# Gate-up's two plain sets turned token-major, one small store moved, another scheduler model

## The chip, the cores and the metric

The kernel runs on one core of a Trainium2 chip. The metric is the device time of one launch in microseconds (us). Before the change three executions took 2731.93, 2734.11 and 2739.36 us; their median, 2734.11 us, is the number to beat. One further execution was profiled; its span, from the first to the last instruction, is 2731.7 us.

## The reference, cut to what matters

One decoder layer over 512 tokens of width 2048, in float32. Two token mixers (latent attention and a gated delta rule) come first. The change is in the channel mixer behind them:

```python
x = x + gt_a * mix
h = _rmsnorm(x, norm_ffn[l]) * (1.0 + sc_f) + sh_f
gate, up = jnp.split(h @ w_gate_up[l], 2, axis=-1)      # 5632 columns each
x = x + gt_f * ((jax.nn.silu(gate) * up) @ w_down[l])
return _rmsnorm(x, final_norm)
```

`gt_f` is a vector of 2048 gates, one per output channel.

## The kernel before, in words

**Precision.** Every product of two float32 matrices is made of three TensorE matmuls over operands split into a high and a low part (`fp32r`): high by high, high by low, low by high. ScalarE casts the high part (`hi`), VectorE subtracts to get the low part (`lo`), for weights and activations alike. `halves` (L263, L264) does it for plain weights, `hilo` (L239, L240) for activations.

**Order of the work.** A layer is a stream of `Unit`s, each with a load (SyncE's DMA queue), a split (ScalarE and VectorE), a list of matmuls, and hooks `pre` and `post`. `Driver.run` takes unit after unit; before a unit's matmuls (after them, where the unit is marked `late`) it splits the next ones, so that two split units lie ahead (`AHEAD`), and loads further ahead (`LOADS = 4` loaded units, 2 in the large sets). Beside the units run generators, called chains, that make the next stage's operands. After each `GROUP = 12` matmuls, each counted with its unit's `weight`, `pump` takes every chain one step further. `hold` at the end of a set delays that by one group. Instructions of SyncE, GpSimd and TensorE stay in program order (`PINNED`). VectorE's and ScalarE's order is chosen when the program is built, by a scheduler that plays the program through a timing model of its own.

**Buffers.** Tiles of 128 x 512 come from a pool of 68 slots (`S`), raw weights from 5 buffers of 128 x 1024, `hi` and `lo` from 4 each, and PSUM gives 8 banks of 128 x 512 float32.

**Gate-up.** The 5632 feature columns of gate and of up are cut into 11 x 512. The first 512 are two *plain* sets (`gu0`, `gu1`) of 256 gate columns and the 256 up columns that belong to them; the other ten are *large* sets (`big(s)`, s = 1 to 10), made with a Strassen-like scheme of seven products, `m1` to `m7`, over sums of weights and sums of activations.

- Input of all: `h2T[h][q]`, high and low part, for token halves h = 0, 1 (256 tokens) and q = 0 to 7 (two blocks of 128 of the 2048 input channels). The chain `h2_gen(h)` makes one q in two steps (L1752, L1753, then `hilo`); the one for h = 1 runs during `gu0`.
- `gu0` walks over the 16 channel blocks twice, once for each token half, loading and splitting its weights twice. It is feature-major: the weight block (128 x 128) is the stationary operand, the 256 tokens of a half the moving one, so each matmul has 256 columns; a bank holds 128 features x 512 tokens. `gu1` (`gu_both(1)`) walks once over the channel blocks and takes both token halves with each, again in matmuls of 256 columns. Each set has 384 matmuls.
- `gu_done` reads the banks at the end of a set: SiLU of the gate on ScalarE (L2152), times up on VectorE (L2154), into two tiles `sl`, which GpSimd's queue stores to `f_dram[s, h]`.
- During `gu1` the chain `combine` (L1780 and `hilo`) makes the sums of activations that the large sets need: for each of four q, four subtractions or additions and four splits. `comb[q]` is due at unit 2q of the first large set.
- A large set has 16 units. Units 0 to 7 run four products, units 8 to 15 the other three. Its matmuls are token-major: 128 tokens of an activation are stationary, 512 weight columns move, each matmul has 512 columns. Units 0 to 7 form sums of weights on VectorE (L1826, 128 x 1024 and 128 x 512) ahead of the split (L1847 on ScalarE, L1848 on VectorE) and store one of them to `s_dram`; units 8 to 15 load it again.
- A large set's result is token-major, but the down projection needs features on partitions. The result, four tiles in `turning`, is turned by TensorE during units 9 to 12 of the next set (`turned_a`: 16 transposes in four groups of four, one ScalarE copy per group at L1957, one store to `f_dram` per group). During the first large set `turning` is empty, and `turned_a` does nothing.

**The gate's store.** `side(g_dram..., gt_ffn)` writes the 2048 gates from a tile of 128 x 16 to memory, in an order in which no two neighbours of a partition are neighbours in memory: 4 bytes at a time. It is on GpSimd's queue, behind the unit stream's `gu1`. Its reader is a load at the kernel's very end (`row<-g_dram`).

Of the kernel before, what the change touches and what calls it, by code (L numbers as in the profile page):

```python
# [171 lines left out]
def block_kernel(ctx: ExitStack, tc: tile.TileContext, a: dict, out, out_t):  # L172
# [1967 lines left out]
    def gu_done(s, ps):  # L2140

        f = {}

        def done(j, h):
            if h == 0:
                return
            for h in range(2):
                fs, v = slice(256 * (j % 2), 256 * (j % 2) + 256), ps[j][:, 256 * h:256 * h + 256]
                if j < 2:
                    if j == 0:  # L2150
                        f[h] = S("sl")
                    nc.scalar.activation(f[h][:, fs], v, AF.Silu)  # L2152
                else:
                    nc.vector.tensor_tensor(f[h][:, fs], f[h][:, fs], v, ALU.mult)  # L2154
                if j == 3:
                    side(f_dram[s, h], f[h][:])
        return done

    def gu_both(s):

        st = {}

        def unit(k0):
            box = {}

            def start():
                box["raw"] = fetch(gu_loads(s)(k0, 2), 512, 2)

            def split():
                box["w"] = halves(box.pop("raw"), 512, 2)  # L2170

            def pre():
                if k0 == 0:
                    st["ps"] = [PS(f"gu{s}") for _ in range(4)]
                    st["done"] = gu_done(s, st["ps"])

            def after(j, h):
                st["done"](j, h)

            mms = []  # L2180
            for kk in range(2):
                k = k0 + kk
                for j in range(4):
                    for h in range(2):
                        for n, (wi, xi) in enumerate(((0, 0), (0, 1), (1, 0))):
                            mms.append(lambda kk=kk, k=k, j=j, h=h, n=n, wi=wi, xi=xi: mm(
                                st["ps"][j][:, 256 * h:256 * h + 256], box["w"][wi][:, kk, tok(j)], half_k(h2T[h][k // 2], k)[xi],
                                start=k == 0 and h == 0 and n == 0, stop=k == KT - 1 and n == 2, skip_group_check=True))
                        if k == KT - 1:
                            mms[-1] = lambda m=mms[-1], j=j, h=h: (m(), after(j, h))  # L2190
# [26 lines left out]
    def ffn():  # L2217
        def gu0():
            us, st = [], {}

            def done(ps):
                done_ = gu_done(0, ps)
                for j in range(4):
                    for h in range(2):
                        done_(j, h)

            for h in range(2):
                half = fm_set("gu0", gu_loads(0), 512, KT, lambda k, h=h: half_k(h2T[h][k // 2], k), done if h else None, st=st,
                              cols=slice(256 * h, 256 * h + 256), alone=True)
# [5 lines left out]
                us.append(half)  # L2235
# [6 lines left out]
            with_pre(us[0], start)  # L2242
            return us[0] + us[1]
# [285 lines left out]
```

## Time and profile before

| | |
|---|---|
| median of three executions | 2734.11 us (2731.93 to 2739.36) |
| profiled execution | span 2731.7 us |
| instructions | 41089, of which 15304 matmuls and as many weight loads |
| loads of `w_gate_up` in the large sets | 400 of 256 KB, 3.6 us from issue to landing (median) |
| stage of the plain sets | 1379.9 to 1473.4 us |
| the ten large sets | 1473.4 to about 2250 us |
| mean granted TensorE clock | 0.998 |

How to read it. "Busy" for the matmul engine (PE) includes modelled ends, so the pace of PE is better read from the chain of work that ended last: a row such as "start, duration, PE name xN" is N matmuls in a row, and duration over N is the pace. PE is TensorE's matmuls, PEld its weight loads, DVE VectorE, ACT ScalarE, POOL GpSimd, SP SyncE; a "q" behind a name is the engine's sequencer. In a table by stretches of time each row has a stretch, its length, the busy time (and count) of PE, PEld, DVE, ACT and POOL, the granted clock of TensorE as a share, the mean busy share of the 16 DMA engines, and GB/s moved. All matmuls are recorded at the line of a helper, L155, so they are told apart by the name of their output tile: `gu` for the plain sets, `m` for the products, `aT` for transposes.

### The profile page before, as it was taken

How to read it: one execution, taken by the hardware profiler on the slowest of the kernel's cores; microseconds unless marked ns; L12 is line 12 of the kernel's file. 1: busy time of each engine (PE TensorE's matmuls, PEld its weight loads, DVE VectorE, ACT ScalarE, POOL GpSimd, SP SyncE). 2: the span in 40 equal slices, each digit the busy share in tenths (PEclk: the TensorE clock that was granted, in tenths of full speed). 3: DMA queues.
4: the chain of work that ended last, by engine and by line, in shares of the span. 5: the costliest groups of instructions: out<-in, count | busy, mean ns of one | idle time of the engine just before them, and what ended most of it. 6: DMA issues, size and time to landing. Idle time of an engine off the chain costs nothing.

```text
span 2731.7 us, 41089 instructions
## 1 busy us (share of the span) xinstructions
PE 2705.7 (99%) x15304; PEld 2351.8 (86%) x15304; DVE 2098.3 (77%) x3361; ACT 1204.9 (44%) x1717; POOL 258.8 (9%) x361
## 2 busy tenths in 40 slices
PE   9999999999999999999999999999999999999998
PEld 7888788888888888889999888888888888998997
DVE  8784656677977886788787877778787777877877
ACT  3443432442344343234473444444444446446445
POOL 0000011102101000001000000000000103113113
PEclk9999999999999999999999999999999999999999
DMA  9896455646666978725854556665655668569565
GB/s 364 302 357 215 143 177 173 190 144 185 198 187 194 315 253 313 258 78 131 268 185 136 195 201 208 204 208 198 212 190 198 214 212 208 132 194 202 126 190 178
DMA packets 315489, 562.20 MB, mean 206 GB/s; under 512 B 40772, under 2 KB 120916, under 8 KB 315288
## 3 DMA queue, kind: packets, MB, share of 16 engines
q1 hardware_dynamic: 264776, 458.99, 51.6%
q0 software_dynamic: 31872, 74.76, 10.6%
q10 hardware_dynamic: 18640, 25.83, 2.7%
q8 instruction: 120, 1.97, 0.3%
q14 instruction: 81, 0.66, 0.1%
HBM read 476.62 MB, written 83.89 MB: 205 GB/s over the span
## 4 chain that ended last, share of the span: by engine, by line
PE 90%; DVE 4%; DMA 3%; issue 2%; ACT 1%; SPq 0%; DVEq 0%; ACTq 0%; POOL 0%
PE m L155 41%; PE gb L155 6%; PE v L155 4%; PE gu L155 3%; PE z L155 3%; PE ya L155 3%; PE k L155 3%; PE q L155 3%; PE yb L155 3%; PE dn L155 3%; PE s L155 3%; PE ckv L155 2%; PE cq L155 2%; PE wo L155 1%; PE qk L155 1%
## 5 line engine op out<-in xcount | busy, mean ns | idle before, releaser
L263 ACT CAST hi<-raw 128x1024 fp32r<-128x1024 f32 x249 | 258.8, 1041 | 538.9 <-DMA raw<-in_w_in_dram 164.9
L264 DVE TENSOR_TENSOR lo<-raw,hi 128x1024 fp32r<-128x1024 f32 x249 | 302.6, 1216 | 202.4 <-ACT hi L263 197.6
L1847 ACT CAST hi<-raws 128x512 fp32r<-128x512 f32 (+1 forms) x240 | 218.6, 911 | 328.0 <-PE m L155 269.2
L1848 DVE TENSOR_TENSOR lo<-raws,hi 128x512 fp32r<-128x512 f32 (+1 forms) x240 | 247.4, 1042 | 83.9 <-ACT hi L1847 83.6
L155 PE MATMUL m<-xh,lo 128*128 128x256 f32 x1088 | 308.4, 283 | 1.3 <-DVE lo L2023 1.3
L155 PE MATMUL m<-xh,hi 128*128 128x256 f32 x1088 | 308.1, 283 | 1.5 <-ACT hi L2022 1.5
L155 PE MATMUL m<-xl,hi 128*128 128x256 f32 x1088 | 307.9, 283 | 0.0
L449 DVE CUSTOM_DVE_ANT_0 rawm<-rawm,cbc 128x1024 f32<-128x1024 f32 x192 | 232.1, 1230 | 2.0 <-DMA rawm<-in_w_mod_dram 1.7
L155 PEld LDWEIGHTS m<-xh,lo 128*128 128x128 f32 x1088 | 208.8, 192 | 2.0 <-DVE lo L2023 1.9
L155 PEld LDWEIGHTS m<-xh,hi 128*128 128x128 f32 x1088 | 208.9, 192 | 1.7 <-ACT hi L2022 1.7
L155 PEld LDWEIGHTS m<-xl,hi 128*128 128x128 f32 x1088 | 208.9, 192 | 0.1
L155 PE MATMUL m<-hi,h2h 128*128 128x512 f32 x480 | 190.1, 396 | 0.0
L155 PE MATMUL m<-hi,h2l 128*128 128x512 f32 x480 | 187.2, 390 | 0.0
L155 PE MATMUL m<-lo,h2h 128*128 128x512 f32 x480 | 187.2, 390 | 0.0
L2022 ACT CAST hi<-sums 128x1024 fp32r<-128x1024 f32 x88 | 92.2, 1048 | 134.4 <-PE m L155 102.4
L2023 DVE TENSOR_TENSOR lo<-sums,hi 128x1024 fp32r<-128x1024 f32 x88 | 107.4, 1220 | 45.5 <-ACT hi L2022 45.4
L1847 ACT CAST hi<-sums 128x1024 fp32r<-128x1024 f32 x80 | 84.2, 1053 | 109.4 <-PE m L155 104.5
L1848 DVE TENSOR_TENSOR lo<-sums,hi 128x1024 fp32r<-128x1024 f32 x80 | 97.6, 1220 | 26.7 <-ACT hi L1847 26.1
L155 PEld LDWEIGHTS m<-hi,h2l 128*128 128x128 f32 x480 | 90.1, 188 | 19.0
L155 PEld LDWEIGHTS m<-hi,h2h 128*128 128x128 f32 x480 | 90.2, 188 | 18.5 <-DVE euvw L1865 0.7
L155 PEld LDWEIGHTS m<-lo,h2h 128*128 128x128 f32 x480 | 90.3, 188 | 17.5
L2022 ACT CAST hi<-raws 128x768 fp32r<-128x768 f32 x88 | 73.4, 835 | 66.8 <-PE m L155 48.1
(581 smaller groups left out, 7418.3 us busy)
## 6 DMA issues: line engine op xcount, KB each, us to landing
raws<-in_w_gate_up_dram SPq DMA_DIRECT2D x400, 256.0 KB, 3.6
rawm<-in_w_mod_dram SPq DMA_DIRECT2D x192, 512.0 KB, 5.4
raw<-in_w_in_dram SPq DMA_DIRECT2D x143, 512.0 KB, 4.6
raws<-in_w_down_dram SPq DMA_DIRECT2D x128, 256.0 KB, 3.9
s_dram<-raws POOLq DMA_DIRECT2D x80, 256.0 KB, 2.3
raws<-s_dram SPq DMA_DIRECT2D x80, 256.0 KB, 3.3
rawa<-in_w_in_dram SPq DMA_DIRECT2D x32, 512.0 KB, 4.6
raws<-in_w_o_dram SPq DMA_DIRECT2D x48, 256.0 KB, 3.1
```

The costliest lines, as they stand in the source:

```text
L155: return self.tc.keep_in_program_order(f(*args, **kwargs))
L263: nc.scalar.copy(hi[:], raw[:])
L264: (lo_eng or nc.vector).tensor_tensor(lo[:], raw[:], hi[:].bitcast(F32), ALU.subtract)
L449: r = nc.vector.tensor_tensor_reduce(raw, raw, c, 1.0, 0.0, ALU.mult, ALU.add, parts[:, k, half:half + 1])
L1847: nc.scalar.copy(hi[:], src)
L1848: nc.vector.tensor_tensor(lo[:], src, hi[:].bitcast(F32), ALU.subtract)
L2022: nc.scalar.copy(hi[:], src)
L2023: nc.vector.tensor_tensor(lo[:], src, hi[:].bitcast(F32), ALU.subtract)
```

## The change

Four things are changed.

1. The two plain sets are token-major (`gu_tokens`): the stationary operand is 128 tokens of `h2T`, the moving one 512 weight columns (256 gate, 256 up), so a set has 192 matmuls of 512 columns. A bank holds 128 tokens x 256 gate and 256 up columns, and `gu_read` makes SiLU times up from one bank. The results go to four tiles `first_tiles` (one for each 128 tokens; set 0 fills columns 0 to 255, set 1 columns 256 to 511), which are put on `turning` behind `gu1`; so `turned_a` turns and stores them during the first large set, with 16 transposes that were not there. The stores of `sl` are gone. The last unit of each half of `gu0` is now `late`, and the `hold` behind `gu0` is gone.
2. These units have `weight=2`: the chains step after 6 of their matmuls instead of 12.
3. The gate's store is issued ahead of unit 0 of the fifth large set, instead of behind `gu1`'s units.
4. `TileContext` is told `schedule_with_timeline_sim=True`: the order on VectorE and ScalarE, over the whole kernel, is chosen with another timing model.

```diff
-    def gu_done(s, ps):
-        f = {}
-        def done(j, h):
-            if h == 0:
-                return
-            for h in range(2):
-                fs, v = slice(256 * (j % 2), 256 * (j % 2) + 256), ps[j][:, 256 * h:256 * h + 256]
-                if j < 2:
-                    if j == 0:
-                        f[h] = S("sl")
-                    nc.scalar.activation(f[h][:, fs], v, AF.Silu)
-                else:
-                    nc.vector.tensor_tensor(f[h][:, fs], f[h][:, fs], v, ALU.mult)
-                if j == 3:
-                    side(f_dram[s, h], f[h][:])
-        return done
-    def gu_both(s):
-        st = {}
+    first_tiles = {}
+    def gu_read(s, ht, bank):
+        if s == 0:
+            first_tiles[ht] = S("g0")
+        o, g = first_tiles[ht][:, 256 * s:256 * s + 256], S("sl")
+        nc.scalar.activation(g[:, 0:256], bank[:, 0:256], AF.Silu)
+        nc.vector.tensor_tensor(o, g[:, 0:256], bank[:, 256:512], ALU.mult)
+    def gu_tokens(s, hts):
+        banks = {}
...
-            mms = []
-            for kk in range(2):
-                k = k0 + kk
-                for j in range(4):
-                    for h in range(2):
-                        for n, (wi, xi) in enumerate(((0, 0), (0, 1), (1, 0))):
-                            mms.append(lambda kk=kk, k=k, j=j, h=h, n=n, wi=wi, xi=xi: mm(
-                                st["ps"][j][:, 256 * h:256 * h + 256], box["w"][wi][:, kk, tok(j)], half_k(h2T[h][k // 2], k)[xi],
...
+            def one(kk, h, t, n, xi, wi):
+                k = k0 + kk
+                mm(banks[h, t][:], half_k(h2T[h][k // 2], k)[xi][:, tok(t)], box["w"][wi][:, kk, :],
+                   start=k == 0 and n == 0, stop=k == KT - 1 and n == 2)
+                if k == KT - 1 and n == 2:
+                    gu_read(s, (h, t), banks.pop((h, t)))
+            mms = [lambda kk=kk, h=h, t=t, n=n, xi=xi, wi=wi: one(kk, h, t, n, xi, wi)
+                   for kk in range(2) for h, t in hts for n, (xi, wi) in enumerate(((0, 0), (0, 1), (1, 0)))]
             def post():
-                if k0 + 2 == KT:
+                if k0 + 2 == KT and s == 1:
                     for q in range(4):
                         h2T[1][q] = None
-            return Unit(start, split, mms, pre, post, late=k0 + 2 == KT)
+                    turning.append((0, first_tiles))
+            return Unit(start, split, mms, pre, post, weight=2, alone=s == 0, late=k0 + 2 == KT)
...
-                half = fm_set("gu0", gu_loads(0), 512, KT, lambda k, h=h: half_k(h2T[h][k // 2], k), done if h else None, st=st,
-                              cols=slice(256 * h, 256 * h + 256), alone=True)
+                half = gu_tokens(0, [(h, t) for t in range(2)])
...
-        yield from with_pre(gu_both(1), lambda: xc.append(drv.add(combine())))
-        side(g_dram.rearrange("(k p) -> p k", p=P), gt_ffn[:])
+        both = gu_tokens(1, [(h, t) for h in range(2) for t in range(2)])
+        yield from with_pre(both, lambda: xc.append(drv.add(combine())))
...
             for i, u in enumerate(big(s)):
+                if (s, i) == (5, 0):
+                    with_pre([u], lambda: side(g_dram.rearrange("(k p) -> p k", p=P), gt_ffn[:]))
...
-    with tile.TileContext(nc) as tc:
+    with tile.TileContext(nc, schedule_with_timeline_sim=True) as tc:
```

More of the change, by code (lines that the diff above doesn't have):

```diff
@@ L2173, in pre @@
                 if k0 == 0:
[L2174 to L2178, printed above, removed]
[L2180 to L2190 removed]
+                    for ht in hts:
+                        banks[ht] = PS(f"gu{s}")
+            def one(kk, h, t, n, xi, wi):
+                k = k0 + kk
+                mm(banks[h, t][:], half_k(h2T[h][k // 2], k)[xi][:, tok(t)], box["w"][wi][:, kk, :],
[4 more added lines that the diff above has]
+                   for kk in range(2) for h, t in hts for n, (xi, wi) in enumerate(((0, 0), (0, 1), (1, 0)))]
             def post():
[L2193 removed]
+                if k0 + 2 == KT and s == 1:
                     for q in range(4):
                         h2T[1][q] = None
[L2197 removed]
+                    turning.append((0, first_tiles))
+            return Unit(start, split, mms, pre, post, weight=2, alone=s == 0, late=k0 + 2 == KT)
         return [unit(k0) for k0 in range(0, KT, 2)]
@@ L2218, in gu0 @@
         def gu0():
[L2219 to L2225, printed above, removed]
+            us = []
             for h in range(2):
-                half = fm_set("gu0", gu_loads(0), 512, KT, lambda k, h=h: half_k(h2T[h][k // 2], k), done if h else None, st=st,
-                              cols=slice(256 * h, 256 * h + 256), alone=True)
+                half = gu_tokens(0, [(h, t) for t in range(2)])
                 for i, u in enumerate(half):
@@ L2234, in gu0 @@
                     with_pre([u], ahead)
-                us.append(half)
+                us += half
             def start():
@@ L2241, in start @@
                 start_h2(1)()
-            with_pre(us[0], start)
-            return us[0] + us[1]
+            with_pre(us, start)
+            return us
         def reload_a(k):
```

## The prediction

> **What bounds the kernel now.** I read the page first, then the chain of waits that ended last in order of time, then single stretches.
>
> ```profile
> span 2731.7 us, 41089 instructions
> PE 2705.7 (99%) x15304; PEld 2351.8 (86%) x15304; DVE 2098.3 (77%) x3361; ACT 1204.9 (44%) x1717; POOL 258.8 (9%) x361
> PEclk9999999999999999999999999999999999999999
> PE 90%; DVE 4%; DMA 3%; issue 2%; ACT 1%; SPq 0%; DVEq 0%; ACTq 0%; POOL 0%
> ```
>
> The first of these lines is the span, the second the busy times; PE is at 99% and 90% of the chain, the clock is full almost throughout. Since a busy PE may still be a slow PE, pace is what counts. These are rows of the chain, from five stretches:
>
> ```profile
> 234.12 43.52 PE k L155 x192
> 699.99 35.36 PE ckv L155 x156
> 1379.88 7.20 PE gu L155 x60
> 1387.08 0.79 PE hss L155 x8
> 1387.87 8.74 PE gu L155 x72
> 1396.60 0.43 PE hbc L155 x2
> 1397.04 76.31 PE gu L155 x636
> 1426.90 46.20 PE gu L155 x385
> 1473.35 26.77 PE m L155 x118
> 1601.24 0.44 PE aT L155 x4
> 1601.68 4.12 PE m L155 x18
> 1771.34 0.44 PE aT L155 x4
> ```
>
> The plain sets (`gu`) run from 1379.88 to 1473.35 us without a gap; only eight `hss` and two `hbc` matmuls of a chain stand between. So TensorE bounds this stage, and matmul time taken out of it should come off the end, as long as what feeds TensorE keeps up.
>
> **The change, part by part.**
>
> *Matmuls of 512 columns for those of 256.* Now: 93.47 us (1473.35 less 1379.88) less 0.79 and 0.43 is 92.25 us for 768 matmuls, 120.1 ns each. After: 384 of 512 columns. The pace of that shape is 43.52/192 = 226.7 ns (`k`) and 35.36/156 = 226.7 ns (`ckv`, which is token-major like the new sets). 384 x 226.7 = 87.05 us. Gain: **5.2 us**. Two of 256 cost 240.2 ns against 226.7 for one of 512, so each matmul has some 13.5 ns that don't depend on its columns.
>
> Against this stands a rule. The Trainium skill (TensorE: Matmul & The Clock Gate, section Back-to-back issue gap) puts the isolated gap at columns over 2.4 GHz plus 2.5 ns. By it the halved count is worth 384 x 2.5 ns, an estimate of 1.0 us, which the transposes below would eat up. The two paces above disagree with it, and the measurement decides.
>
> *Sixteen transposes more*, in the first large set, where `turned_a` was empty: four groups at 0.44 us (the `aT` rows) make **1.8 us**, all on TensorE.
>
> *The reading of the banks.*
>
> ```profile
> L2152 ACT ACTIVATE sl<-gu x8: 378/384/405, 1426.7 to 1472.2; 128x256 f32<-128x256 f32 x8
> L2154 DVE TENSOR_TENSOR sl<-sl,gu x8: 411/413/422, 1427.1 to 1473.8; 128x256 f32<-128x256 f32 x8
> L1957 ACT COPY f<-aT x28: 577/577/579, 1602.2 to 2084.7; 128x512 f32<-128x512 f32 x28
> L155 POOL DMA_DIRECT2D f_dram<-f x28: 540/540/543, 1603.1 to 2085.6; - x28
> ```
>
> Eight SiLU and eight products stay as many and as wide; four of the first half of `gu0` move ahead by half a set. New are four copies of 0.58 us on ScalarE and four stores of 0.54 us on GpSimd's queue; four stores of `sl` go. They stand in units 9 to 12 of the first large set, where `s_dram` isn't stored, and the next large sets do the same without a gap in the chain. Nothing on the path.
>
> *VectorE under a shorter stage.* These are stretches of the trace (columns: length, PE, PEld, DVE, ACT, POOL, clock, DMA share, GB/s):
>
> ```profile
> 1358.00:1366.00 8.00, 8.00 (x55) 8.00 (x56) 5.25 (x16) 2.10 (x2) 0.00 (x0) 0.79 0.66 211
> 1380.00:1404.00 24.00, 24.00 (x201) 23.95 (x201) 21.93 (x45) 17.80 (x28) 0.00 (x0) 1.00 0.64 198
> 1404.00:1427.00 23.00, 23.00 (x194) 23.00 (x194) 19.20 (x28) 18.58 (x29) 0.00 (x0) 1.00 0.57 183
> 1433.00:1443.00 10.00, 10.00 (x86) 10.00 (x85) 8.70 (x13) 5.68 (x9) 0.00 (x0) 1.00 0.46 26
> 1473.00:1516.00 43.00, 43.00 (x192) 35.65 (x192) 31.28 (x36) 17.04 (x19) 4.31 (x8) 1.00 0.59 196
> 1785.00:1824.00 39.00, 39.00 (x173) 32.28 (x172) 32.32 (x35) 15.30 (x17) 3.25 (x6) 1.00 0.70 230
> ```
>
> The first half of `gu0` will take 96 x 226.7 ns + 1.2 = 23.0 us instead of 24. VectorE is busy 21.9 us in it, and two products (0.8 us) come in: 22.7 of 23.0. That is the tightest point of the change. The cover is the two units already split and the chain's lead. I take 0; if the cover is gone it costs up to 2 us here. The weight of 2 keeps the chains at two steps in a `gu0` unit and four in a `gu1` unit as before, so it costs nothing by itself; the dropped `hold` moves one step by 12 matmuls.
>
> *The gate's store* sends 2048 pieces of 4 bytes. In the stretch from 1433 to 1443 us, right behind its issue at 1429.6, the DMA engines are 46% busy and move 26 GB/s. What that did to loads, against the place it moves to (issues from 1431.4 to 1437, and from 1783 to 1800):
>
> ```profile
> L155 POOL DMA_DIRECT2D g_dram<-gt_ffn x1: 1177/1177/1177, 1429.6 to 1429.6; - x1
> raws<-in_w_gate_up_dram SPq DMA_DIRECT2D x6, 256.0 KB, 12.9
> raws<-in_w_gate_up_dram SPq DMA_DIRECT2D x11, 256.0 KB, 3.1
> 1788.81 5.91 SPq L155 DMA_DIRECT2D raws<-in_w_gate_up_dram  x6
> 1791.57 0.68 DVE L1826 TENSOR_TENSOR raws<-sums,raws 128x512 f32<-128x512 f32 x1
> 1793.91 1.22 DVE L1826 TENSOR_TENSOR sums<-raws,raws 128x1024 f32<-128x1024 f32 x1
> L1847 ACT CAST hi<-raws 128x1024 fp32r<-128x1024 f32 x160 | 168.7, 1055 | 286.9 <-PE m L155 230.4 <-DVE raws L1826 43.3 <-PE gu L155 4.7
> L1848 DVE TENSOR_TENSOR lo<-raws,hi 128x1024 fp32r<-128x1024 f32 x160 | 195.3, 1220 | 79.0 <-ACT hi L1847 78.8
> ```
>
> Six loads landed after 12.9 us instead of 3.1, 9.8 us late, and nobody noticed, because they were the first large set's and TensorE had half of `gu1` to go. Taking the store away there gains 0. In the fifth large set it comes on GpSimd's queue behind unit 2's `s_dram` store, so near 1789 us; behind it wait unit 3's store (its reader is unit 11) and, in the DMA engines, unit 4's three loads, issued from 1788.81. Unit 4's sums start at 1793.91, so those loads would land near 1803.5. Set 5 begins 54 matmuls (three units of 18) behind 1771.78, at 1784.0, and unit 4 is 96 further, at 1805.8. From landing to the unit's second matmul VectorE and ScalarE need 1.22 + 0.68 + 1.06 + 1.22 = 4.2 us: 1807.7, less 0.2 for the first matmul. A stall of some **1.7 us**; bounds 0 (the loads are sliced in between) and 9.8 (no lead at all).
>
> The Trainium skill (DMA: Bandwidth & Descriptors, section Queues, rings and completion order) lets each DMA engine alternate between the queues that have work, packet by packet. By that rule the loads would keep moving beside the store, and this term would be near 0. The 26 GB/s and 12.9 us do not agree with it.
>
> *The other scheduler model* can't be seen in this trace. It removes nothing; it reorders 3361 instructions of VectorE and 1717 of ScalarE. The gain is bounded by the time that TensorE waits now, and by the tail:
>
> ```profile
> PE cb L155 <- DMA crow<-in_c_dram: 3.1, 1, 3.1
> PE hss L155 <- DVE sq L1444: 2.2, 1, 2.2
> ...
> PE cq L155 <- ACT sz L962: 0.9, 1, 0.9
> 2697.00:2731.70 34.70, 23.79 (x123) 20.18 (x121) 26.37 (x73) 11.90 (x29) 5.82 (x8) 0.89 0.34 122
> ```
>
> Seven rows of waits of TensorE, from 3.1 down to 0.9 us, come to about 12 us, of which the 3.1 is a first load; the `hss` wait cost 2.2 and then, at a clock of 0.79 over 8 us, 1.7 more. The tail is 35 us of VectorE and ScalarE work with 26.4 us of VectorE busy. So some 10 us can be won. Lost can be more: in the first half of a large set VectorE is busy 32.3 of 39 us. I take 0, as the row nearest (no gap in 93 us of `gu`, next to VectorE at 91%) says the order now is already one that TensorE doesn't feel; ends -10 and +20.
>
> Sum: -5.2 + 1.8 + 1.7 + 0 = -1.7 us. On the span that gives 2730.0; the median is 2.4 us above the span, and the runs spread by 7.4, so I put it on the median: **2732 us**.
>
> **The rivals.**
>
> 1. *The new order fills waits*: the `hss` wait with its slow clock (3.9 us) and some 4 of the tail's 8 idle VectorE us: 2732 - 8 = 2724. For it: these are the only places where order reaches the end. Against: the tail is a chain of short dependent steps.
> 2. *The new order starves the large sets* (the other side). Place: units 0 to 7 of each of the ten large sets. Mechanism: VectorE in strict order behind an instruction that waits for a load or for TensorE, while sums for the next unit are due; the lead is what unit 4 above has (about 8 us between landing and deadline with 4.4 us of VectorE work per unit). Price 1.5 us a set, 15 in all: 2747. It decides from 1 us a set, which makes the change slower by over 0.3%. For it: the 32.3 of 39 us. Against: over the whole span VectorE is at 77%, and a step that slips has units 8 to 15 of the set to catch up in.
> 3. *The slots run out.* `first_tiles` holds 4 of 68 slots throughout `gu1`, where `h2T` holds 32 and the finished `comb` grows to 32: the last quarter of `combine` has to wait for the slots that `gu1`'s end frees, and its 8 instructions of 0.68 us (5.5 us) fall into the first large set. VectorE has 11.7 us idle in 1473 to 1516, but not all before unit 2: up to 5.5 us, 2737.
> 4. *The store stops TensorE for the whole delay*: 9.8 instead of 1.7 us: 2740.
> 5. *The wide matmul is no cheaper*: the pace of 512 turns out at twice that of 256, so only the transposes and the store remain: +3.5, 2737. The paces above speak against it.
>
> **How the numbers follow.** My sum 0.37, rival 1 0.16, rival 2 0.25, rival 3 0.13, rival 4 0.07, rival 5 0.02. 0.3% is 8.2 us, about what three runs of this kernel (spread 7.4) can tell from no change: below 2725.9 is faster, above 2742.3 slower. Faster 0.16 (rival 1), slower 0.25 (rival 2), same 0.59 (the rest). The range 2722 to 2748 leaves out under half of rival 1 and about half of rival 2, some 0.18. The sum's own range, with the store between 0 and 3 and VectorE up to 2, is 2730 to 2735.
>
> **What would show it.** `gu` rows of some 226.7 ns a matmul, the stage at 88.3 us instead of 93.5; four `aT` groups in the first large set; DMA at some 26 GB/s for 10 us behind 1785 us, with loads there at 12 to 13 us and a gap of TensorE near unit 4 of the fifth set. Wrong would make it: TensorE waits named for `lo` or `hi` of `gu` or `m` that are not there now, a clock below 1.00 in the large sets, or a tail shorter or longer than 35 us by several.

## The result, and the profile after

The changed kernel takes 2798.36 us (median; 2792.76 to 2801.24) against 2736.28 us before: a ratio of 1.0228, with a 95% interval of 1.0211 to 1.0245. It is 62 us slower where I forecast 2732 us, and outside the range. The profiled execution has a span of 2791.0 us, 59.3 more than before.

The page of the changed kernel, its span, its busy times and the shares of the chain that ended last:

```profile
span 2791.0 us, 40381 instructions
PE 2724.9 (98%) x14936; PEld 2341.3 (84%) x14936; DVE 2092.0 (75%) x3361; ACT 1204.6 (43%) x1721; POOL 257.5 (9%) x361
PE 64%; issue 17%; DVE 8%; DMA 7%; ACT 1%; POOL 1%; SPq 1%; DVEq 0%; POOLq 0%; ACTq 0%
```

VectorE and ScalarE do what they did before, to a few us. What has gone is the unbroken line of TensorE: it held 90% of the chain, and holds 64% now. The waits of TensorE (who waited for whom: us in total, times, the longest):

```profile
PE m L155 <- DVE euvw L1865: 15.6, 20, 2.7
PE cT L155 <- DVE ckv L1001: 7.7, 1, 7.7
PE ga L155 <- DVE lo L264: 5.8, 2, 4.2
PE m L155 <- DVE lo L1848: 5.2, 1, 5.2
```

None of these was among the rows before, but for 1.7 us of `ga`. They lie all over the kernel. All rows of this view together come to some 53 us, against 15 before. Much of what the waits leave of the 59.3 us is clock. At some of the waits the granted clock falls to half and stays there behind them, as at the end of the 7.7 us for `ckv` (stretch, length, PE, PEld, DVE, ACT, POOL, clock, DMA share, GB/s):

```profile
771.90:778.70 6.80, 4.15 (x11) 2.94 (x12) 5.89 (x13) 0.69 (x1) 0.00 (x0) 0.50 1.07 247
```

The mean granted clock is 0.991 over 2791.0 us and was 0.998 over 2731.7. That makes 25.1 us of clock withheld against 5.5, so slow clock is up to some 20 us of the loss. This is an estimate and an upper bound, since clock that is withheld while TensorE waits costs nothing.

The table gives where the time goes, from the first matmul of `q` (190.4 us before), of the plain sets `gu` (1379.7), of the first large set (1473.2), of the down projection `dn` (2252.4) and of its last part `dnl` (2669.8), each in the profiled execution; every number is that stretch's length less its length before, in us. The kernels of the experiments stand below the changed one. A profiled execution can lie off its kernel's median, most of all in the row "old model, store back" (2753.67 us against 2742.45). Only the down projection gains, 2 to 5 us, wherever the new model is on.

| kernel | to `q` | to `gu` | plain sets | large sets | `dn` | rest |
|---|---|---|---|---|---|---|
| changed | 12.5 | 11.6 | 2.5 | 34.6 | -4.3 | 2.3 |
| new model alone | 12.1 | 10.7 | 4.4 | 31.9 | -4.6 | 2.1 |
| old model | 2.5 | 2.5 | 0.9 | 9.8 | 0.1 | 2.4 |
| old model, weight 1 | -0.5 | 3.3 | 3.2 | 11.4 | -1.2 | 0.7 |
| old model, store back | 2.9 | 8.4 | 0.9 | 2.8 | 0.9 | 4.3 |
| store back, late read | -0.6 | 2.9 | -3.2 | 3.4 | 0.9 | 0.8 |
| late read, `hbc` one group later | -0.3 | 6.3 | -2.7 | 2.4 | -1.1 | 1.1 |
| late read, `hbc` two groups later | 0.0 | 3.6 | -3.1 | 2.1 | -1.2 | 0.7 |
| changed, sums tied | 12.3 | 12.2 | 2.6 | 15.0 | -4.5 | 4.1 |
| changed, additions only | 13.0 | 14.4 | 0.9 | 28.6 | -3.7 | 2.2 |
| changed, products only | 14.3 | 14.0 | 0.9 | 23.5 | -3.7 | 2.2 |
| changed, `acc` tied | 12.7 | 11.1 | 0.9 | 38.0 | -2.0 | 2.1 |
| changed, repaired | 12.8 | 10.1 | -0.1 | 6.5 | -3.8 | 2.2 |
| repaired, head tied | 2.8 | 13.6 | -0.2 | 6.5 | -3.5 | 2.2 |

### The profile page after: what moved, and what is told of

Read it like the earlier page. It is cut to its first block, busy times and chain, and to the rows that moved or that the text cites. A ratio compares the mean times of both kernels' runs of the same rounds, so it can differ in the third digit from the quotient of the medians.

```text
span 2791.0 us, 40381 instructions
## 1 busy us (share of the span) xinstructions
PE 2724.9 (98%) x14936; PEld 2341.3 (84%) x14936; DVE 2092.0 (75%) x3361; ACT 1204.6 (43%) x1721; POOL 257.5 (9%) x361
## 3 DMA queue, kind: packets, MB, share of 16 engines
q0 software_dynamic: 31872, 74.76, 10.1%
## 4 chain that ended last, share of the span: by engine, by line
PE 64%; issue 17%; DVE 8%; DMA 7%; ACT 1%; POOL 1%; SPq 1%; DVEq 0%; POOLq 0%; ACTq 0%
PE m L155 20%; PE gb L155 5%; PE v L155 4%; DMA raws<-in_w_gate_up_dram 3%; PE s L155 3%; PE k L155 3%; PE dn L155 3%; PE q L155 3%; PE yb L155 3%; PE gu L155 3%; PE z L155 3%; PE ga L155 2%; PE wo L155 2%; PE ckv L155 2%; DVE lo L1848 2%
## 5 line engine op out<-in xcount | busy, mean ns | idle before, releaser
L1848 DVE TENSOR_TENSOR lo<-raws,hi 128x512 fp32r<-128x512 f32 (+1 forms) x240 | 248.0, 1043 | 85.1 <-ACT hi L1847 84.2
L1826 DVE TENSOR_TENSOR sums<-raws,raws 128x1024 f32<-128x1024 f32 x80 | 97.7, 1221 | 28.3 <-DMA raws<-in_w_gate_up_dram 23.1
L1826 DVE TENSOR_TENSOR raws<-raws,raws 128x512 f32<-128x512 f32 x80 | 55.2, 690 | 78.7 <-DMA raws<-in_w_gate_up_dram 78.4
```

Of the source, the lines that this page charges most:

```text
L1826: add = lambda o, x, y: nc.vector.tensor_tensor(o, x, y, ALU.add)
L1848: nc.vector.tensor_tensor(lo[:], src, hi[:].bitcast(F32), ALU.subtract)
```

## The experiments

Theory A: the order that the new scheduler model makes costs nearly all of the 62 us. Theory B, its rival: the token-major sets do, by starving what lies around them. Where a later expectation uses a letter anew, it says what it stands for.

### Parting the change

**The changed kernel with the old scheduler model.**

```diff
-    with tile.TileContext(nc, schedule_with_timeline_sim=True) as tc:
+    with tile.TileContext(nc) as tc:
```

> The kernel after with the scheduler model of before; the token-major sets, the weight of 2 and the moved store stay. Theory A (the other order on VectorE and ScalarE costs nearly all of the 62 us): 2727 to 2737 us, TensorE without gaps before the plain sets, the plain sets' stage at 88 to 89 us, large sets at some 78 us, a stall of 0 to 5 us in the fifth. Theory B (the token-major sets start it: late chains or slots leave the large sets without a lead): 2765 us or more, large sets at 80 us or more.

**The kernel before with the new scheduler model alone**, the same line the other way round.

> The kernel before with the other scheduler model alone. Theory A: 2785 to 2800 us, with the same gaps of TensorE in the head, near 770 us and at unit 8 of the large sets. Theory B: at most 2765 us, since the 24 us ahead of the plain sets come without the token-major sets, and the rest (some 33 us in the large sets) does not.

**The old model, and the store back at its place in the program**, behind the units of `gu1`. In time it doesn't come back to where it was, as the next section shows.

```diff
         yield from with_pre(both, lambda: xc.append(drv.add(combine())))
+        side(g_dram.rearrange("(k p) -> p k", p=P), gt_ffn[:])
...
-                if (s, i) == (5, 0):
-                    with_pre([u], lambda: side(g_dram.rearrange("(k p) -> p k", p=P), gt_ffn[:]))
```

> As e1, with the gate's store back behind the second plain set. Theory A with a store that delays loads of the fifth large set: 1 to 5 us under e1, and the fifth set as long as its neighbours. If the store is hidden in the fifth set with the old order: within 1 us of e1.

**The old model, and weight 1 in the plain sets.**

```diff
-            return Unit(start, split, mms, pre, post, weight=2, alone=s == 0, late=k0 + 2 == KT)
+            return Unit(start, split, mms, pre, post, weight=1, alone=s == 0, late=k0 + 2 == KT)
```

> As e1, with each matmul of the plain sets counted once, so that the chains step half as often beside them. If the chains' pace matters: up to 10 us over e1, with TensorE waiting for h2 in the first plain set or for x6, x7 or x5 in the first large set. If the forced steps ahead of each unit suffice: within 2 us of e1.

Measured, beside 2734.25 us before: old model 2749.21 us (ratio 1.005, 1.0037 to 1.0063); new model alone 2789.16 us (1.0203, 1.0189 to 1.0216); store back 2742.45 us (1.0035, 1.0022 to 1.0049); weight 1 2750.41 us (1.0052, 1.004 to 1.0064).

So the new model by itself costs 55 us of the 62, and theory A holds in the main. But it doesn't hold for the rest: the old model should have brought 2727 to 2737 us and stands at 2749. The structure costs 15 us where I had it win 1.7. The two don't add: 55 and 15 make 70, so beside the new model the structure costs 7. Moving the store back takes 6.8 us off the 15 (2749.21 less 2742.45, a little above its expectation). Weight 1 makes no difference to the median that these runs can tell, which was expected; in its profiled execution the plain sets are 2.3 us longer, with waits of 4.4 us for `h2h`, so there the chains' pace does show. That leaves 8 us over the kernel before, in the plain sets and ahead of them.

### The plain sets under the old model

In the chain that ended last of the kernel with the old model (start, duration, what) the plain sets no longer run through:

```profile
1402.01 0.40 DVE diag L1467 x2
...
1402.46 0.70 PE hbc L155 x2
1403.16 15.02 PE gu L155 x66
...
1420.09 0.63 ACT h2h L239
...
1420.76 58.63 PE gu L155 x252
```

There are two breaks: `hbc` waits 1.5 us for `diag`, and near 1420 us `gu` waits 2.6 us for `h2h`. Ahead of the second break ScalarE does this (the timeline of ScalarE, same kernel, and below it VectorE's):

```profile
1413.84 1.28 ACT L2147 ACT_TABLE_LOAD   x1
1415.13 0.38 ACT L2147 ACTIVATE sl<-gu 128x256 f32<-128x256 f32 x1
1416.44 0.37 ACT L2147 ACTIVATE sl<-gu 128x256 f32<-128x256 f32 x1
```

```profile
1412.59 0.69 DVE L240 TENSOR_TENSOR h2l<-h2f,h2h 128x512 fp32r<-128x512 f32 x1
1417.71 0.41 DVE L2148 TENSOR_TENSOR g<-sl,gu 128x256 f32<-128x256 f32 x1
1418.04 0.87 DVE L1752 SCALAR_TENSOR_TENSOR h2f<-x,s_ffn,hbc 128x256 f32<-128x256 f32 x2
```

This is the reading of the first half's two banks. It needs a function that isn't loaded (1.28 us), the SiLUs come behind the half's last matmuls, the products for the SiLUs, and the next step of `h2_gen(1)` stands behind the products: 5.45 us lie between one `q` of that chain and the next. The Trainium skill (ScalarE: Activation LUTs, section What ACT_TABLE_LOAD costs) gives 1283 ns for the load and another 1380 ns of drain; the trace shows the 1.28 us, and the SiLU starts 0.01 us behind it.

Theory R: that reading is the cause; theory V: VectorE is full in any case. First the reading alone is put off to the end of the second half:

```diff
-                    gu_read(s, (h, t), banks.pop((h, t)))
+                    unread.append((s, (h, t), banks.pop((h, t))))
+                    if s or h:
+                        while unread:
+                            gu_read(*unread.pop(0))
```

> The kernel with the old scheduler model and the store at its old place, and one more edit: the banks of the first half of gu0 are read at the end of the second half, not in the middle of the stage. Theory R (the read in the middle stops the chain h2_gen for h = 1: in the trace of the kernel with the store back TensorE waits 2.6 us for h2h near 1418 us, and the SiLUs, a ScalarE row of 1.28 us without tiles and the products stand ahead of the next step of that chain): that wait goes, the stage of the plain sets gets 3 to 5 us shorter, the median 2737 to 2740. Theory V (VectorE is simply full in the first half of gu0, whatever is read when): the wait stays or moves by a unit, the stage within 1 us, the median within 2 us of the 2742.45 of the kernel with the store back.

Then, on top of it, `hbc` one group later, and in a third kernel two groups:

```diff
-        yield 6 if h else 4
+        yield 7 if h else 4
```

> As the kernel with the late reading, and h2_gen(1) waits one group longer between the diagonal and its spreading (yield 7 for yield 6), so that six matmuls of gu more stand ahead of hbc. Theory R: both waits of the stage (1.5 us for diag, 2.6 us for h2h) are gone, the stage of the plain sets has 88 to 90 us from first to last matmul instead of 94.2, the median 2733 to 2737, so within 3 us of the kernel before, since the 1.8 us of transposes and the 2.3 us of the first large set stay. Theory V: the wait for diag goes, but the chain starts later and the wait for h2h comes back larger: stage 92 us or more, median 2740 or more.

> The old scheduler model, the store at its old place, the banks of gu0's first half read at the end of the second, and two groups more ahead of hbc (yield 8 for yield 6). Theory R (only the chain's stalls stand between the structure and its 384 x 226.7 ns): no wait of hbc, the plain sets take 88 to 89 us from first to last matmul, the median 2732 to 2736. Theory V (VectorE is too full there for the shorter stage): a wait for h2h or h2l comes instead, 90 us or more, 2737 to 2742.

Measured: late read 2738.81 us (ratio 1.0016, 1.0006 to 1.0027), one group later 2739.04 us (1.0014, 1.0005 to 1.0024), two groups later 2738.95 us (1.0014, 1.0005 to 1.0023). The stage from the first `gu` to the first product takes 94.4 us with the store back, 90.3 with the late read, 90.7 and 90.4 with `hbc` moved too. So the reading in the middle is 4.1 us in the profiled executions and 3.6 in the medians, as theory R says; how much of it is the function's loading, this edit doesn't tell, as it moves the whole reading. The wait of `hbc` for `diag`, still 1.5 us with the late read, goes when `hbc` is moved, but the stage is as long without it as with it. The two later kernels miss the 88 to 90 and 88 to 89 us of theory R. The last one lies where theory V put it (90 us or more, 2737 to 2742), and its sign of that, a wait for `h2h` or `h2l`, is there too. It doesn't show in the waits of PE, but in those of the weight loads (PEld), which load `h2h` and `h2l` as the stationary operand, here of the last kernel from 1383 to 1474 us:

```profile
PEld gu L155 <- DVE h2l L240: 2.2, 7, 0.4
PEld gu L155 <- ACT h2h L239: 1.1, 4, 0.3
```

```profile
1406.64 0.19 PEld L155 LDWEIGHTS gu<-hi,h2h 128*128 128x128 f32 x1 [0.26 <-ACT h2h L239]
...
1407.37 0.19 PEld L155 LDWEIGHTS gu<-hi,h2l 128*128 128x128 f32 x1 [0.43 <-DVE h2l L240]
```

With the late read alone these rows aren't there. In the last kernel the chain `h2_gen(1)` starts later, and in the second half of `gu0` several of its `q` are made only just as they are due. A weight load that otherwise runs under the matmul before it then comes late, and the matmuls around it start 330 to 390 ns apart instead of 226.7: at four places, three in a row, 1.5 us in all. That is as much as the wait for `diag` that went. So the wait has moved: an early `hbc` makes TensorE wait for `diag`, and a late one leaves the chain no lead. Theory V's reason, a VectorE that is too full, isn't shown by this.

All three kernels stay 3.2 to 3.5 us above the kernel before in the median, although from the first `gu` on their profiled executions are within 2 us of it. The rest lies ahead of `gu` there, in the mixers' last projection. With `hbc` one group later TensorE waits 3.2 us there; VectorE's wait for the loads of `w_o`, in that kernel and before:

```profile
DVE sums L2014 <- DMA raws<-in_w_o_dram: 13.6, 3, 9.2
```

```profile
DVE sums L2014 <- DMA raws<-in_w_o_dram: 6.2, 3, 2.1
```

These loads land late in four of the kernels with the old model and not in the two with the store in the fifth set. The reason is the gate's store. GpSimd's timeline before, and in the kernel with `hbc` one group later:

```profile
1428.50 1.08 POOL L155 DMA_DIRECT2D f_dram<-sl  x2 [122.70 <-DVE sl L2154]
1429.57 1.18 POOL L155 DMA_DIRECT2D g_dram<-gt_ffn  x1
```

```profile
1305.86 1.19 POOL L155 DMA_DIRECT2D g_dram<-gt_ffn  x1
```

Before, the store stood behind the stores of `sl`, which waited for the end of `gu0`. In the token-major kernels those are gone, and at its old place in the program nothing holds it: it is issued some 120 us earlier, between the loads of `w_o`. The loads that were issued there land after 12.2 us, where with the store in the fifth set they take 5.3 (issues from 1302 to 1309, and from 1305 to 1312 of the kernel with the old model):

```profile
raws<-in_w_o_dram SPq DMA_DIRECT2D x2, 256.0 KB, 12.2
raws<-in_w_o_dram SPq DMA_DIRECT2D x2, 256.0 KB, 5.3
```

The same holds for all six kernels with the store back, the two under the new model included (issued between 1304 and 1326 us). So "store back" isn't the state before: it takes the store out of the fifth set, and puts 1 to 5 us into the last projection (from its first matmul to the first of `wo`, against before). A kernel in which the store is held until behind `gu0` wasn't run. With it the three kernels would be about level with the kernel before, an estimate from their profiled executions from the first `gu` on (1.9 us above, 0.3 and 1.5 below).

### The store in the fifth set

With the old model the fifth large set takes 85.1 us from its first matmul to the next set's, where the others take 78.1 (the first two 78.5 and 79.0). These are the waits of TensorE in that set, three stretches of it (start and end, length, PE, PEld, DVE, ACT, POOL, clock, DMA share, GB/s) and the loads that were issued from 1800 to 1806 us, of the kernel with the old model:

```profile
PE m L155 <- DVE lo L1848: 2.8, 1, 2.8
PE m L155 <- DVE euvw L1865: 2.0, 1, 2.0
```

```profile
1804.00:1808.00 4.00, 4.00 (x19) 3.31 (x18) 3.54 (x5) 2.07 (x2) 0.54 (x1) 1.00 0.52 9
1808.00:1812.00 4.00, 4.00 (x19) 3.32 (x18) 0.00 (x0) 1.05 (x1) 0.00 (x0) 1.00 0.61 78
1816.00:1824.00 8.00, 6.21 (x20) 4.92 (x21) 8.00 (x9) 2.88 (x3) 1.08 (x2) 0.79 0.43 144
```

```profile
raws<-in_w_gate_up_dram SPq DMA_DIRECT2D x3, 256.0 KB, 11.2
```

The DMA engines are half busy and move 9 GB/s; three loads take 11.2 us; VectorE stands still from 1808 to 1812, TensorE a little later. Behind the wait the clock is 0.79 on average over 8 us, and at unit 8 the set waits once more. With the store out of the set it takes 78.1 us.

### The large sets under the new model

In the changed kernel a large set takes 79.5 to 83.1 us (the fifth 87.0), with the new model alone 77.5 to 82.9, before 78.1. VectorE's waits for loads of the large sets, before and after:

```profile
DVE raws L1826 <- DMA raws<-in_w_gate_up_dram: 60.1, 49, 2.2
DVE sums L1826 <- DMA raws<-in_w_gate_up_dram: 3.0, 4, 1.3
```

```profile
DVE raws L1826 <- DMA raws<-in_w_gate_up_dram: 78.4, 53, 4.0
DVE sums L1826 <- DMA raws<-in_w_gate_up_dram: 23.1, 27, 7.7
```

Where TensorE pays is unit 8 (VectorE's timeline in the third set of the changed kernel; below it the matmul that waited):

```profile
1701.14 0.69 DVE L1826 TENSOR_TENSOR raws<-raws,raws 128x512 f32<-128x512 f32 x1 [2.26 <-DMA raws<-in_w_gate_up_dram]
1703.35 0.69 DVE L1826 TENSOR_TENSOR raws<-raws,raws 128x512 f32<-128x512 f32 x1 [1.51 <-DMA raws<-in_w_gate_up_dram]
1705.09 1.28 DVE L1871 TENSOR_TENSOR euvw<-euvw,m 128x512 f32<-128x512 f32 x2
1707.49 1.88 DVE L1865 TENSOR_TENSOR euvw<-euvw,m 128x512 f32<-128x512 f32 x3
```

```profile
1707.02 0.50 PE L155 MATMUL m<-hi,h2h 128*128 128x512 f32 x1 [1.42 <-DVE euvw L1865]
```

The same place before:

```profile
1665.63 0.69 DVE L1826 TENSOR_TENSOR raws<-raws,raws 128x512 f32<-128x512 f32 x1 [1.15 <-DMA raws<-in_w_gate_up_dram]
1667.50 0.69 DVE L1826 TENSOR_TENSOR raws<-raws,raws 128x512 f32<-128x512 f32 x1 [1.18 <-DMA raws<-in_w_gate_up_dram]
```

Additions of units 8 to 12 stand ahead of the reads of the banks (L1871, L1865), and did so before too; but there they waited less for their loads, 1.15 and 1.18 us, and TensorE didn't wait. What differs is what makes the loads late. At the set's start the four products of the finished set (L1896) come bunched, in the fourth set 4.4, 6.1, 6.7 and 8.5 us behind its first matmul on `x6`, where before they came at 3.5, 8.1, 12.7 and 17.4; the additions behind them, and so the loads that wait for their buffers, are late from there on. To take them apart, instructions are tied: each is put behind the VectorE instruction that stands before it in the program, so that it can't be moved ahead of it.

```diff
+        vec = Ordered(tc, nc.vector)
...
-            add = lambda o, x, y: nc.vector.tensor_tensor(o, x, y, ALU.add)
+            add = lambda o, x, y: vec.tensor_tensor(o, x, y, ALU.add)
...
-                    nc.vector.scalar_tensor_tensor(a_[:], a_[:], -1.0, (v, up1)[h][t], op0=ALU.mult, op1=ALU.mult)
+                    vec.scalar_tensor_tensor(a_[:], a_[:], -1.0, (v, up1)[h][t], op0=ALU.mult, op1=ALU.mult)
```

Both tied:

> The changed kernel, new scheduler model and all, with two kinds of VectorE instructions of the large sets kept in the order of the program among themselves: the additions of weights (L1826) and the products of the finished set (L1896). Theory B (the new model bunches the four products in units 0 and 1, which holds back the additions, so the loads behind them are issued later, and at unit 8 TensorE waits for bank m7): the large sets go back from about 80.3 us to 78 to 79 us, the time from the first plain set to the down projection gets 12 to 20 us shorter, the median 2778 to 2787. Theory S (the loss is spread over the order as a whole, or over ScalarE): periods stay at 80 to 81 us, the median within 4 us of 2798.

A second kernel ties the reads of the banks (L1865, L1871) as well. Its expectation below names the additions alone; that is not what ran, and it tells nothing between its two cases.

> The changed kernel with the additions of weights (L1826) alone kept in the order of the program among themselves. Theory B: as the products aren't held, they stay bunched and little is won: periods of 80 us, the median within 5 us of 2798. If instead the order of the additions among themselves is the cause: periods of 78 to 79 us, 2778 to 2787, as with both.

The additions alone, and the products alone:

> The changed kernel, new scheduler model, with the additions of weights of the large sets (L1826) alone tied behind the VectorE instruction that stands before each in the program; the products of the finished set (L1896) stay bunched in units 0 and 1. In the changed kernel five additions of units 8 to 12 stand ahead of the reads of the banks (L1871, L1865) at unit 8, and each waits for its loads; here they stand behind those reads. Theory B (bunched products make the loads late): nothing is undone, periods stay near 80 us, the median is 2790 or more. Theory H (additions that wait for loads hold up the reads of the banks): periods of 78 to 79 us, the median 2772 to 2780, as with both tied.

> The mirror image: the products of the finished set (L1896) alone are tied, so they are spread over units 0 to 3 again, and the five additions stay ahead of the reads of the banks, as they stand in the kernel before too. Theory B: periods of 78 to 79 us, the median 2772 to 2785. Theory H: periods near 80 us, the median within 5 us of 2798.

Measured: both 2774.71 us (ratio 1.0146, 1.0129 to 1.0163), four kinds 2774.12 us (1.0143, 1.0128 to 1.0158), additions alone 2789.02 us (1.0199, 1.0184 to 1.0215), products alone 2785.0 us (1.0184, 1.0167 to 1.0201). The sets take 78.6 us with both (the fifth, with the store, 86.8), 80.1 with the additions alone, 78.3 to 81.6 with the products alone. (With one of them tied the fifth set, with the store, takes 89 us.) Neither theory alone is right: of 23.7 us the additions bring 9.3 and the products 13.4. The kernel before differs by up to 2 us between the sessions of these runs; against it, it is 23.0 us for both, 7.5 for the additions and 11.5 for the products, so together they bring more than the sum. The waits of TensorE in the large sets say why, first with the additions tied, then with the products tied (lines two further down than in the kernel):

```profile
PE m L155 <- DVE lo L1850: 14.3, 10, 7.5
PE m L155 <- DVE euvw L1867: 2.7, 9, 0.5
```

```profile
PE m L155 <- DVE euvw L1867: 9.3, 7, 2.7
PE m L155 <- DVE lo L1850: 5.7, 1, 5.7
```

With the additions behind the reads of the banks the wait for the banks falls from 15.6 to 2.7 us, but bunched products still hold up the additions, and the wait moves to `lo`. With the products spread the `lo` wait is left only in the fifth set, behind the store, and part of the sets still wait for the banks. Each order costs something without the other.

### The stages ahead

The largest single wait of the changed kernel is 7.7 us for `ckv`: the nine short dependent steps of a root have an independent sum (`acc`) put between nearly each two. The sum and the scaling by the root are tied:

```diff
-                        nc.vector.scalar_tensor_tensor(acc[:], raw[:, kk, :], cs, acc[:], op0=ALU.mult, op1=ALU.add)
+                        kept.scalar_tensor_tensor(acc[:], raw[:, kk, :], cs, acc[:], op0=ALU.mult, op1=ALU.add)
...
-                    nc.vector.tensor_scalar(cs[t][:], cs[t][:], y[:, t:t + 1], None, op0=ALU.mult)
+                    kept.tensor_scalar(cs[t][:], cs[t][:], y[:, t:t + 1], None, op0=ALU.mult)
```

> The changed kernel with the sums of the shift vector (acc, L396 and L398) and the scaling by the root (L1001) tied behind the VectorE instruction that stands before each in the program. In the changed kernel TensorE waits 7.7 us for ckv near 766 us: the nine short dependent steps of the root (rs, 0.15 us each) have an acc of 0.75 us put between nearly each two. Theory A (the order alone, each stall at its place): this wait falls below 1.5 us, everything behind it comes 5 to 8 us earlier, the median is 2788 to 2794. Rival (the work put off is due soon behind, so the time comes back as another wait): the wait goes, but the attention's first matmuls start no more than 3 us earlier, and the median is within 3 us of 2798.

Measured: 2795.9 us (ratio 1.0222, 1.0207 to 1.0237), the rival's median. The wait is gone and the attention's first matmuls start 8 us earlier, as theory A says and the rival doesn't; but the attention takes 5.5 us of it back, with a wait of 4.0 us for `knl` that the changed kernel doesn't have, and by the plain sets, which start 0.4 us earlier, nearly all is gone.

All repairs at once, under the new model:

> The new scheduler model kept, with every repair at once: additions and products of the large sets tied, acc and L1001 tied, the store of the gate back behind the plain sets, the banks of the first half of gu0 read at the end of the second, and h2_gen(1) one group later. If the causes add up (24 us for the large sets, 5 to 8 for ckv, 7 for the store, 4 to 6 for the plain sets, from 2798): 2752 to 2760, and what is left over the kernel before, some 20 us, is order in the stages ahead of the plain sets. If they overlap: 2762 or more.

Measured: 2761.99 us (ratio 1.0101, 1.0086 to 1.0116), by 2 us outside what adding up would give, and at the lower edge of "overlap". The large sets take 78.6 us each; most of what is left is the 23 us ahead of the plain sets. More than half of them lie ahead of `q`. VectorE's timeline near there, in the changed kernel, and the same place before:

```profile
164.12 10.02 DVE L513 SCALAR_TENSOR_TENSOR xT<-xT,s_mix,r_all 128x512 f32<-128x512 f32 x15
174.06 1.22 DVE L264 TENSOR_TENSOR lo<-raw,hi 128x1024 fp32r<-128x1024 f32 x1
```

```profile
162.49 2.07 DVE L513 SCALAR_TENSOR_TENSOR xT<-xT,s_mix,r_all 128x512 f32<-128x512 f32 x3
164.48 1.22 DVE L264 TENSOR_TENSOR lo<-raw,hi 128x1024 fp32r<-128x1024 f32 x1
```

Fifteen products for a later stage stand ahead of the `lo` that the next matmuls need. In the last kernel these are tied, `hl` too, and ScalarE's first casts are put behind the SiLUs of `cbc`:

```diff
+        silu = spread_c()
...
+        with tc.issue_after(silu.ins):
+            prepare(0)
...
+        tc.keep_in_program_order(nc.vector.scalar_tensor_tensor(x[:], x[:], sc, r_all[:], op0=ALU.mult, op1=ALU.mult))
```

> The repaired kernel with the new scheduler model, and its head tied as well: prepare(0) behind the four SiLUs of cbc on ScalarE, and on VectorE the products hl (L508), xT (L513) and their low parts (L516) each behind the instruction that stands before it in the program. In the changed kernel fifteen xT products stand in a row, 10.02 us of VectorE, ahead of the lo that TensorE waits 4.2 us for; in the kernel before they stand in threes, twos and ones. Theory A (work put off is bunched ahead of what is due, stall by stall): the start of q, 12.8 us later than before in the repaired kernel, comes back to 1 to 5 us, the plain sets start 8 to 11 us earlier, the median 2750 to 2755. Rival (what the head wins is given back in the attention, as the 8 us of ckv were): q starts earlier, the plain sets do not, the median 2758 to 2763.

Measured: 2756.58 us (ratio 1.0073, 1.0059 to 1.0086), between the two cases. `q` starts 2.8 us later than before instead of 12.8, as theory A says; of these 10 us 6.4 reach the plain sets in the profile, where theory A had 8 to 11, and 5.4 the median. What is left under the new model, some 21 us, is 2 to 6 us in each of several stages; 3.5 of them lie in the mixers' last projection, where the store now stands, and the others are not traced further. No kernel here beats the kernel before.

## Why the prediction was wrong

**The other scheduler model: the step that failed.** I took 0, with ends of -10 and +20; it costs 55 us. The reason given was that TensorE has no gap in 93 us next to a VectorE at 91%, so that the order now "is one that TensorE doesn't feel". That is true of the order that was there, and says nothing of another. Two rows of the trace before could have told more. VectorE already waited 60.1 us at 49 additions of the large sets, so it stood in strict order behind loads, and the reads of the banks stood behind these additions; it went well because these waits were short enough (at most 2.2 us) not to reach TensorE. And the upper end of 20 was drawn from the large sets alone, while the model orders every stage: 24 of the 59.3 us arise ahead of the plain sets. No sum of waits alone would have been enough either: up to some 20 us of the loss is the slow clock behind them, which I had counted only for `hss`.

**Rival 2 had the place and the mechanism** in the large sets, VectorE in strict order behind an instruction that waits for a load. I priced it at 1.5 us a set; it is 1.4 to 5 us. It doesn't sit where I put it, in units 0 to 7, but at unit 8, where the banks are read, and it begins with the products at the set's start. The catching up in units 8 to 15 that spoke against it doesn't happen: the stall is there.

**512 columns for 256.** 384 times 226.7 ns was to win 5.2 us. The pace is right where nothing disturbs it; the stage wins 3.1 us when the reading is put off, loses 0.9 with the old model and 2.5 as changed. What is missing isn't in the width of the matmuls but in the next two steps, 4 and 2 us.

**The reading of the banks.** "Nothing on the path" counted instructions and their lengths, and these are right. What I named and did not follow is that four of them "move ahead by half a set": into the middle of a chain that runs at most one step ahead of TensorE, with a function to be loaded. That is 4.1 us.

**VectorE under a shorter stage.** I took 0, and up to 2 us "if the cover is gone". It is gone: the 1.5 us for `diag` are in that half, and when `hbc` is moved to spare them, the weight loads wait for `h2h` and `h2l` instead. The stage stays at 90.3 to 90.7 us where 88.3 was forecast. The place and the price were right, the choice of 0 was not.

**The transposes** cost what was forecast: four groups of 0.44 us in the first large set (at 1531.5 to 1545.2 us of the kernel with the old model).

**The store.** The place and the mechanism were right, the size wasn't: 7.0 us against 1.7, inside the bounds of 0 and 9.8. The loads took 11.2 us, near the 12.9 assumed. The first wait is 2.8 us, 1.1 more; what the sum left out is the slow clock behind it (0.79 over 8 us, 1.7 us, which I had counted for `hss`) and a second wait of 2 us at unit 8, where the set stood with less lead than it had before. The Trainium skill (DMA: Bandwidth & Descriptors, section Queues, rings and completion order) has the queues served in turn, packet by packet. The loads did keep moving, but at 9 GB/s and then 78: the rule gives no speed, and my step from it to "near 0" doesn't hold.

**The weight** costs nothing, as forecast. Rival 1 (waits filled) did not come at its places: the `hss` wait stays (2.4 us), and the last stretch grew by 2.3. Rival 3 (slots) did not: with the late read the first large set takes 78.2, 78.6 and 79.6 us in three kernels, 76.2 before; 1.8 of the growth is transposes, and the longest wait of TensorE in that set is 1.2 us, for a read of a bank (`euvw`) and not for sums of activations. Rival 5 did not. Rival 4 priced the store at 9.8 and was nearer than the sum.

## What to carry to other kernels

A change to how instructions are ordered is a change to every stage, and a busy engine without gaps tells nothing of how another order would do: look for instructions that wait for loads in an in-order queue, for what stands behind them, and how much lead that has. Work of one kind that is put off (products of the set before, sums for a later stage) does harm when it comes bunched ahead of what the next matmuls need, even where its total is unchanged. When a read of results is moved into the middle of a stage, ask which chain shares its engines there and how far ahead that chain is. An instruction without a wait of its own runs as early as the queue lets it: taking away what stood ahead of it moves it, even where its own line isn't touched.

## What the hardware showed that I had not expected

- Some waits of TensorE cost more than themselves: behind the 2.2 us for `hss` (before) and the 2.8 us of the store the granted clock is 0.79 over 8 us, and from 771.9 us of the changed kernel it is 0.50 for 6.8 us. It isn't every wait: behind the 2.6 us for `h2h` in the plain sets it stays at 1.00.
- The first SiLU behind other functions costs ScalarE 1.28 us of loading, here in the middle of a stage.
- While a store in pieces of 4 bytes runs, the loads of another queue move slowly, at 9 GB/s over one stretch of 4 us, and the DMA engines count as half busy. It delays whatever loads it meets: 12.9, 11.2 and 12.2 us to landing in three places, against 3.1 (in the sets) and 5.3 (`w_o`).
- A weight load that waits for its operand, for as little as 0.26 us, shows in the rows of PEld and not in those of PE, whose matmuls merely start further apart.
